# The opening of a hybrid encoder block: first half of the input in 512 KB pairs and scaled by its norm ahead, modulated forms from ScalarE, adaLN row sums in a PSUM bank a piece ahead

## The chip, the cores and the metric

One of the eight cores of one Trainium2 chip runs the kernel; the other seven are idle. The metric is the time of one execution in microseconds (us), as the median of three runs. A core has five engines that run on their own and wait for one another by semaphores: TensorE (PE in the profile, with its weight loads as PEld), VectorE (DVE), ScalarE (ACT), GpSimd (POOL) and SyncE (SP), which issues nearly all DMAs of this kernel.

## The reference

One encoder block of width 1024 over a sequence of 1024 positions, batch 1, in float32. What the change touches is its first lines: a conditioning vector `c` gives six vectors of 1024 (`ada`), the input is normalised and modulated by two of them, and the result goes through one wide projection.

```python
ada = jax.nn.silu(c) @ w_ada[i] + b_ada[i]
shift1, scale1, gate1, shift2, scale2, gate2 = [t[:, None, :] for t in jnp.split(ada, 6, axis=-1)]

h = rmsnorm(x, g_mix[i]) * (1 + scale1) + shift1
proj = h @ w_in[i]
qa, ka, va, qb, kb, vb, ga, gb = jnp.split(proj, split_at, axis=-1)
...
merged = jax.nn.sigmoid(ga) * ya + jax.nn.sigmoid(gb) * yb
x = x + gate1 * (merged @ w_out[i])
h2 = rmsnorm(x, g_ffn[i]) * (1 + scale2) + shift2
...
return rmsnorm(x, g_final)
```

`rmsnorm` divides each position by the root of the mean of its squares and multiplies by a gain. Behind the projection stand a dilated attention of three patterns, a neighbourhood attention on a 16 x 64 grid, two branch products with sigmoid gates, an output product, and a ConvFFN of 2 x 2816 columns.

## The kernel before, in words

The input comes transposed: `xT` is eight blocks `k` of 128 channels by 1024 positions, and the positions are treated in two halves of 512. Every float32 product is made of three products of rounded parts: an operand is split into a high part `hi` and the rest `lo`, and PE adds hi by hi, hi by lo and lo by hi in one PSUM bank. `split` does this for weights (ScalarE copies the high part, `tensor_tensor` on VectorE or GpSimd subtracts it), `modulate` for the activations.

The opening, which is the first 63 us, does this:

1. Load the first half of the input, `x[0]` (eight tiles of 256 KB), and square it (`square`: ScalarE squares, VectorE adds four tiles into each of two sums). PE sums over the channels by products with a column of ones (`add_sums`, 128 x 1 products), `rstd_of` makes 1/root, and `bcast` spreads it over the partitions of a PSUM bank, `pb`. Idle products of the identity with itself (`warm`) stand between these steps on PE.
2. The adaLN product for the first two vectors is cut into four pieces `q` of 512 columns: two blocks `k` of shift and the same two blocks of scale. A piece of `w_ada` is 1024 rows, eight tiles `t` of 128 rows by 512 columns. Six of the tiles are multiplied by their column of `silu(c)` (`cs`) and added up by VectorE (`ada_rows`, a `tensor_scalar` and five `scalar_tensor_tensor`, in place in the first tile). PE does the other two tiles and the sum over partitions of the added ones, four 128 x 1 products for each (`ada_sums`, into the bank `pada`). `piece_bias` adds the bias and makes `1 + scale` times the gain for two blocks.
3. `modulate` makes, for each block, `t = x * am1 * pb` (VectorE, into a PSUM bank), `hi = t + shift` (ScalarE), `lo = t + shift - hi` (VectorE).
4. As soon as two blocks are there, PE adds their part to two banks of q and k (`qk_products`, 512 columns wide) and to four half banks of v (`v_products`, 256 wide). Then comes the next piece.

Everything in this opening stands in one block with a fixed order (`manual_schedule`): each engine runs its instructions in the order in which the code is written, and so does the SP queue with its loads. What sets the time is therefore which instruction stands ahead of which on an engine. Steps 2 to 4 go once for each of the four pieces, in the loop `for q in range(4)`. Behind it stand the same steps for the second half of the input, `x[1]`, whose norm and modulation lie beside products of the first half.

Buffers: `x[0]` and `x[1]` lie in tiles of the pool `h`, the pieces of `w_ada` in tiles that later hold q and k (`kl`, `qs`, `ks`, `qb`) or in tiles named `wada`. The split weights of q and k come in halves of four blocks (`qk_split(0)`, `qk_split(1)`, from tiles `wraw` into `whi` and `wlo`), and those of v likewise (`v_split`, into `vwh` and `vwl`).

## Time and profile before

| | us |
|---|---|
| median of three runs | 1534.29 (1532.61 to 1536.65) |
| the profiled execution, its own time | 1535.67 |
| its span in the profile | 1533.8 |
| PE busy in the span | 1494.4 (97%) |
| VectorE, ScalarE, GpSimd busy | 994.6, 771.6, 774.2 |
| first product of q and k starts (L84) | 25.84 |
| last of the four pieces ends, the second half of v starts (L244) | 62.74 |
| mean clock granted to PE over the span | 0.99 |

All times inside the execution are us from the start of the span. A row of the timeline gives start, length (of the whole group, where several are merged), engine, line, operation, what it writes and reads, the count, and in brackets the idle time of the engine before it with what ended it. In a row of `x16` at line 153 or 98 each 128 x 1 float32 product counts twice, since PE makes two passes of it. A row of the windows gives the stretch, its length, the busy time of each engine with the number of instructions, the granted PE clock (1.00 is full), the DMA share and GB/s; a row of PE alone has only its own busy time. Products are pipelined: a row of 0.39 for a 512-wide product does not mean that the next one starts 0.39 later.

### The profile page before, as it was taken

Reading aid. Unit: us, or ns where it says so; the run is one execution under the profiler, and the core shown is the slowest. Engines: PE = TensorE matmul, PEld = TensorE weight load, DVE = VectorE, ACT = ScalarE, POOL = GpSimd, SP = SyncE. Lnnn points to the kernel's source line nnn. Section 1 sums busy time; section 2 is a strip of 40 time slices with the busy share of each in tenths; the row PEclk is TensorE's granted clock in tenths of the full one; section 3 lists DMA queues with packets and bytes.
Section 4 is the critical chain, followed back from the end, with each engine's and each line's share of the span. In section 5 each row is a group of like instructions: output and inputs, shape, how many; then the busy total and the mean of one; then the engine's idle time right before and its main releaser. Section 6 shows DMA issues by size and latency. Waiting matters only on the chain.

```text
span 1533.8 us, 21797 instructions
## 1 busy us (share of the span) xinstructions
PE 1494.4 (97%) x7740; PEld 1267.5 (83%) x7740; DVE 994.6 (65%) x1892; ACT 771.6 (50%) x1439; POOL 774.2 (50%) x640
## 2 busy tenths in 40 slices
PE   8999999999999999999999989999999998999998
PEld 7888888889798998878888867888888887778787
DVE  5775357575656655646525798766666668787765
ACT  4331566666656566643335463444444447475542
POOL 1021344443335444512268578676666666779721
PEclk9999999999999999999999999999999999999999
DMA  9567333333625456477644222222222224513313
GB/s 349 191 242 258 93 107 82 108 90 102 185 83 150 128 143 173 149 246 234 213 137 147 88 69 96 82 98 88 85 84 86 86 78 154 191 62 124 117 55 111
DMA packets 112725, 205.77 MB, mean 134 GB/s; under 512 B 40516, under 2 KB 53188, under 8 KB 112580
## 3 DMA queue, kind: packets, MB, share of 16 engines
q1 hardware_dynamic: 112344, 204.12, 41.2%
q8 instruction: 61, 1.00, 0.3%
q14 instruction: 48, 0.39, 0.1%
q10 hardware_dynamic: 272, 0.26, 0.1%
HBM read 159.25 MB, written 42.47 MB: 132 GB/s over the span
## 4 chain that ended last, share of the span: by engine, by line
PE 50%; POOL 8%; DVE 7%; ACT 3%; issue 3%; DMA 3%; DVEq 0%; POOLq 0%; ACTq 0%
PE pj L1204 8%; PE pj L1205 8%; PE pj L1206 8%; PE pj L84 6%; PE pj L86 6%; PE pj L85 6%; POOL wsl L61 2%; DMA wraw<-w_down 2%; PE pj L365 2%; PE O L932 2%; POOL wlo L61 2%; DVE big L1426 1%; PE T L919 1%; PE S L897 1%; DVE kl L340 1%
## 5 line engine op out<-in xcount | busy, mean ns | idle before, releaser
L61 POOL TENSOR_TENSOR wlo<-wraw,whi 128x512 fp32r<-128x512 f32 (+1 forms) x94 | 116.1, 1256 | 173.6 <-ACT whi L57 155.4
L84 PE MATMUL pj<-h,whi 128*128 128x512 f32 x448 | 186.7, 417 | 2.6 <-ACT h L207 2.2
L85 PE MATMUL pj<-h,whi 128*128 128x512 f32 x448 | 176.5, 394 | 2.1 <-DVE h L209 2.1
L86 PE MATMUL pj<-h,wlo 128*128 128x512 f32 x448 | 176.3, 393 | 0.0
L61 POOL TENSOR_TENSOR wsl<-big,wsh 128x512 fp32r<-128x512 f32 (+1 forms) x86 | 116.6, 1376 | 43.4 <-ACT wsh L57 43.4
L639 POOL TENSOR_TENSOR wlo<-wraw,whi 128x512 fp32r<-128x512 f32 x58 | 74.7, 1298 | 118.4 <-ACT whi L638 118.4
L589 DVE TENSOR_TENSOR tl<-T,th 128x512 fp32r<-128x512 f32 (+3 forms) x120 | 77.1, 653 | 72.9 <-ACT th L588 71.4
L581 ACT ACTIVATE P<-P,st 128x256 f32<-128x256 f32 x128 | 64.2, 502 | 95.9 <-DVE st L580 95.9
L1426 DVE SCALAR_TENSOR_TENSOR big<-wc,sm,big 128x256 f32<-128x256 f32 (+1 forms) x129 | 101.0, 827 | 15.1 <-ACT big L1420 15.1
L86 PEld LDWEIGHTS pj<-h,wlo 128*128 128x128 f32 x448 | 84.3, 188 | 18.7
L84 PEld LDWEIGHTS pj<-h,whi 128*128 128x128 f32 x448 | 85.0, 190 | 14.3 <-ACT h L207 2.8
L85 PEld LDWEIGHTS pj<-h,whi 128*128 128x128 f32 x448 | 85.0, 190 | 13.4 <-DVE h L209 3.4
L57 ACT ACTIVATE whi<-wraw 128x1024 fp32r<-128x1024 f32 (+2 forms) x51 | 49.5, 972 | 69.8 <-PE pj L85 26.7
L61 POOL TENSOR_TENSOR wsl<-wraw,wsh 128x384 fp32r<-128x384 f32 (+1 forms) x46 | 53.6, 1184 | 58.4 <-ACT wsh L57 58.3
L910 POOL TENSOR_SCALAR P<-P,stb 128x288 f32<-128x288 f32 (+1 forms) x32 | 40.2, 1255 | 72.2 <-DVE stb L907 64.7
L1426 DVE SCALAR_TENSOR_TENSOR big<-pj,sm,big 128x512 f32<-128x512 f32 (+1 forms) x129 | 66.4, 563 | 15.7 <-ACT big L1420 15.7
L588 ACT ACTIVATE th<-T 128x512 fp32r<-128x512 f32 (+3 forms) x120 | 65.6, 566 | 20.4 <-PE T L919 14.0
L57 ACT ACTIVATE wsh<-big 128x1024 fp32r<-128x1024 f32 (+1 forms) x43 | 42.9, 997 | 57.3 <-POOL big L1155 43.0
L547 POOL TENSOR_TENSOR vv<-vv 128x512 fp32r<-128x512 f32 (+1 forms) x40 | 41.9, 1065 | 47.2 <-ACT vv L546 47.2
L580 DVE CUSTOM_DVE_ANT_0 P<-S,bias 128x256 f32<-128x256 f32 x128 | 48.9, 419 | 21.4 <-PE S L692 17.0
L903 ACT ACTIVATE P<-P,stb 128x288 f32<-128x288 f32 (+1 forms) x64 | 36.4, 569 | 50.3 <-DVE stb L901 50.2
L1225 DVE TENSOR_TENSOR pj<-pj,wc 128x512 f32<-128x512 f32 x33 | 22.9, 695 | 53.1 <-PE pj L1206 53.1
(431 smaller groups left out, 4814.3 us busy)
## 6 DMA issues: line engine op xcount, KB each, us to landing
wraw<-w_in SPq DMA_DIRECT2D x34, 512.0 KB, 4.3
wada<-w_ada SPq DMA_DIRECT2D x31, 512.0 KB, 8.0
big<-w_up SPq DMA_DIRECT2D x22, 512.0 KB, 5.4
wraw<-w_up SPq DMA_DIRECT2D x22, 512.0 KB, 3.7
as<-big SPq DMA_DIRECT2D x22, 512.0 KB, 2.8
big<-as SPq DMA_DIRECT2D x22, 512.0 KB, 6.7
wraw<-w_down SPq DMA_DIRECT2D x24, 384.0 KB, 3.6
gs<-gs SPq DMA_DIRECT2D x32, 256.0 KB, 2.9
```

Of the source, the lines that this page charges most:

```text
L57: act.activation(hi, raw, AF.Copy)
L61: lo_eng.tensor_tensor(lo[:, i:i + step], raw[:, i:i + step], f(hi)[:, i:i + step], OP.subtract)
L84: pe.matmul(psum, whi[:, k0 + k], mhi, start=k == 0, stop=False)
L85: pe.matmul(psum, whi[:, k0 + k], mlo, start=False, stop=False)
L86: pe.matmul(psum, wlo[:, k0 + k], mhi, start=False, stop=k == n - 1)
L588: act.activation(th[:m, :n], pt[:m, :n], AF.Copy)
L589: dve.tensor_tensor(tl[:m, :n], pt[:m, :n], f(th)[:m, :n], OP.subtract)
L639: pool.tensor_tensor(lo[:, i:i + n], raw[:, i:i + n], f(hi)[:, i:i + n], OP.subtract)
L1204: pe.matmul(psum, whi[:, k], bhi, start=j < 4 and k == 0, stop=False, skip_group_check=True)
L1205: pe.matmul(psum, whi[:, k], blo, start=False, stop=False, skip_group_check=True)
L1206: pe.matmul(psum, wlo[:, k], bhi, start=False, stop=k == n - 1, skip_group_check=True)
L1426: dve.scalar_tensor_tensor(y[:, dst], src, wt, y[:, dst], OP.mult, OP.add)
```

## The change

All of it lies in the opening, but for the last load of `x` near the end, which follows the new layout of the input in memory (by halves, then pairs of blocks).

- Loads: the first half of the input comes as four pairs of 512 KB with 4 KB a partition, into tiles of q and k (`ks`, `qb`); the small `idt` and `cs` are issued by ScalarE's queue. Pieces 1 and 2 of `w_ada` go to `wada` and `qb` tiles, piece 3 to eight tiles of the pool `h`, one row tile to a load. The second weights of v (`v_raw1`) are loaded ahead of the second half of the input, into free tiles.
- Norm: two of the eight squares go to PE as they are, so VectorE adds four times instead of six. The broadcast norm `pb` is copied to SBUF (`pbs`), and `x[0]` itself is multiplied by it ahead of the modulation: blocks 0 to 3 by VectorE from PSUM, 4 to 7 by GpSimd from `pbs`.
- Modulation: `scaled` lets ScalarE make both `hi = x * am1 + shift` and the same value unrounded into a PSUM bank; VectorE only subtracts.
- Row sums: `ada_rows` adds in a PSUM bank `acc` and writes the last sum to a tile. Pieces 2 and 3 add seven tiles on VectorE and leave one to PE, and their first two or three rows are added a piece ahead.
- Order on PE: `qk_products` goes hi by hi, hi by lo of the weight, then lo of the activation, over both banks; `v_parts` goes by parts. The row sums of the next piece stand behind 6 of the 24 products of v, where they stood behind 12 (in the first piece they stand around the first 8). The idle products are 14, 2, 4 and 4 where they were 28, 8, 4 and 12.
- Splits: the second halves of the weights of q, k and v go from VectorE to GpSimd, and of the second weights of v one goes to VectorE and one to GpSimd, in the last piece.

```diff
@@ -40,10 +40,10 @@
         return ap.bitcast(FT)
 
     idt = const.tile([128, 128], FT, name="idt")
-    sp.dma_start(idt, ident)
+    nc.scalar.dma_start(idt, ident)
     sm = const.tile([128, 248], FT, name="sm")
     cs = const.tile([128, KT], FT, name="cs")
-    sp.dma_start(cs, c)
+    act.dma_start(cs, c)
     ones = const.tile([128, 1], FT, name="ones")
     dve.memset(ones, 1.0)
     ada = const.tile([128, 48], FT, name="ada")
...
@@ -141,6 +140,12 @@
             wt = wada_tile(j)
             sp.dma_start(wt, w_ada[j][:, t:t + 2])
             rows += [wt[:, i] for i in range(2)]
+        return rows
+
+    def ada_rows_load(j):
+        rows = [h_tile(FT) for _ in range(KT)]
+        for t, w in enumerate(rows):
+            sp.dma_start(w, w_ada[j][:, t])
         return rows
 
     def ada_sums(parts, pa=None, stop=True, n=4, new=None):
@@ -159,20 +164,26 @@
         cc = slice(c0, c0 + n)
         dve.tensor_tensor(ada[:, cc], pa[:, :n], b_ada[:, cc], OP.add)
 
-    def ada_rows(wt, ts, acc=None):
+    def ada_rows(wt, acc, ts, first, last):
 
         for t in ts:
-            if acc is None:
-                acc = wt[t]
-                dve.tensor_scalar(acc, acc, cs[:, t:t + 1], None, OP.mult)
+            col, dst = cs[:, t:t + 1], wt[t] if t == last else acc
+            if t == first:
+                dve.tensor_scalar(dst, wt[t], col, None, OP.mult)
             else:
-                dve.scalar_tensor_tensor(acc, wt[t], cs[:, t:t + 1], acc, OP.mult, OP.add)
-
-    def x_load(hf, ks=range(KT)):
+                dve.scalar_tensor_tensor(dst, wt[t], col, acc, OP.mult, OP.add)
+
+    def x_load(hf):
         x = []
-        for k in ks:
-            x.append(h_tile(FT))
-            sp.dma_start(x[-1], xT[k][:, halves[hf]])
+        for k in range(0, KT, 2):
+            if hf == 0:
+                x2k = qkpool.tile([128, 2, 512], FT, name=("ks", "qb")[k // 6], bufs=(4, 2)[k // 6])
+                sp.dma_start(x2k, xT[hf, k // 2])
+                x += [x2k[:, i] for i in range(2)]
+            else:
+                for i in range(2):
+                    x.append(h_tile(FT))
+                    sp.dma_start(x[-1], xT[hf, k // 2][:, i])
         return x
 
     def sq_accs():
@@ -208,6 +219,14 @@
             if last:
                 dve.scalar_tensor_tensor(*last, OP.add, OP.subtract)
             last = k is not None and (lo, t, b, f(hi))
+
+    def scaled(x, k):
+
+        hi, lo = h[0, k] = h_tile(), h_tile()
+        t, b, g = stage[k % 2], ada[:, k:k + 1], am1[:, k:k + 1]
+        act.activation(hi, x, AF.Identity, bias=b, scale=g)
+        act.activation(t, x, AF.Identity, bias=b, scale=g)
+        return lambda: dve.tensor_tensor(lo, t, f(hi), OP.subtract)
 
     def warm(n, dst, fresh=False):
 
@@ -283,8 +302,21 @@
 
     def qk_products(ks):
         for k in ks:
-            for p, w in zip(qk_psum, qk_w):
-                product(p, w, lambda k: h[0, k], ks=[k])
+            mhi, mlo = h[0, k]
+            for x_, (part, m) in enumerate(((0, mhi), (1, mhi), (0, mlo))):
+                for p, w in zip(qk_psum, qk_w):
+                    pe.matmul(p, w[part][:, k], m, start=k + x_ == 0, stop=k == KT - 1 and x_ == 2)
+
+    def v_parts(hv, sts, ks, parts):
+        whi, wlo = v_w[hv]
+        for part in parts:
+            for st in sts:
+                p = pvs[hv][st]
+                sc = slice(st * 128, st * 128 + 128)
+                for k in ks:
+                    m, w = ((0, whi), (1, whi), (0, wlo))[part]
+                    pe.matmul(p, h[0, k][m][:, sc], w[:, k], start=part + k + st % 2 == 0,
+                              stop=part == 2 and k == KT - 1, skip_group_check=True)
 
     def v_products(hv, sts, ks):
         for st in sts:
@@ -391,53 +423,83 @@
         half_load(qk_raw, (0, 4), 1)
         half_load(v_raw, (8, 9), 1)
         wt.append(ada_load(2))
-        wt.append(ada_load(3))
+        wt.append(ada_rows_load(3))
+        v_raw1 = [qkpool.tile([128, KT, 128], FT, name=n) for n in ("kl", "qs")]
+        for t, raw in enumerate(v_raw1):
+            sp.dma_start(raw, w_in[10 + t])
         x.append(x_load(1))
         qk_w = [[wpool.tile([128, KT, 128], FR, name=n) for n in ("whi", "wlo")] for _ in range(2)]
         v_all = v_tiles()
         v_w = [[t[:, hv] for t in v_all] for hv in range(2)]
         qk_psum = [ps_g.tile([128, 512], FT, name="pj") for _ in range(2)]
-        first = ps_s.tile([128, 512], FT, name="pv", bufs=3)
-        stage = [None, first]
-
-        warm(28, first[:, :128], True)
+        acc = ps_s.tile([128, 512], FT, name="pv", bufs=3)
+        pvs = [v_banks()]
+        idle = pvs[0][0][:, :128]
+
+        warm(14, idle, True)
         accs = sq_accs()
-        square(x[0], accs, range(8), dve)
-        pcol = square_sums(accs, lambda: warm(8, first[:, :128], True))
-        ada_rows(wt[0], range(3))
+        square(x[0], accs, range(6), dve)
+        last = [early.tile([128, 512], FT, name="mt", bufs=3) for _ in range(2)]
+        for sq, xk in zip(last, x[0][6:]):
+            act.activation(sq, xk, AF.Square)
+        pcol = ps_n.tile([128, KT], FT, name="pcol")
+        for i, sq in enumerate(accs + last):
+            add_sums(pcol, sq, i == 0, i == 3)
+            if i == 0:
+                warm(2, idle, True)
+        ada_rows(wt[0], acc, range(3), 0, 5)
         rs = rstd_of(pcol, 4)
-        warm(4, first[:, :128], True)
+        warm(4, idle, True)
         pb = bcast(rs, ps_n, "pbc")
-        ada_rows(wt[0], range(3, 6), wt[0][0])
+        pbs = early.tile([128, 512], FT, name="mt", bufs=3)
+        act.activation(pbs, pb, AF.Copy)
+        ada_rows(wt[0], acc, range(3, 6), 0, 5)
+        for k in range(2):
+            dve.tensor_tensor(x[0][k], x[0][k], pb, OP.mult)
+        qk_split(0, (pool, pool))
         pa = ada_sums([(wt[0][t], cs[:, t:t + 1]) for t in (6, 7)], stop=False)
-        ada_sums([(wt[0][0], ones)], pa)
-        warm(12, first[:, :128], True)
-        stage[0] = ps_n.tile([128, 512], FT, name="pcol")
-        qk_split(0, (pool, pool))
-        v_split(v_raw, (pool, pool), slice(0, 4), v_w[0])
-        pvs = [v_banks()]
+        ada_sums([(wt[0][5], ones)], pa)
+        warm(4, idle, True)
         for q in range(4):
             ks = range(2 * q, 2 * q + 2)
-            if q == 2:
-                v_raw1 = v_load(0, 1)
             piece_bias(q, pa)
-            modulate(x[0], 0, ks, pb)
-            qk_products(ks)
-            if q < 3:
-                ada_rows(wt[q + 1], range(6))
             if q == 0:
-                qk_split(1, (dve, dve))
-                v_split(v_raw, (dve, dve), slice(4, 8), v_w[0])
-            if q == 2:
-                v_split(v_raw1, (dve, dve), slice(0, KT), v_w[1])
+                for k in range(2, 4):
+                    dve.tensor_tensor(x[0][k], x[0][k], pb, OP.mult)
+                stage = [ps_n.tile([128, 512], FT, name=n) for n in ("pcol", "pbc")]
+            low = [scaled(x[0][k], k) for k in ks]
+            if q == 0:
+                v_split(v_raw, (pool, pool), slice(0, 4), v_w[0])
+                for k in range(4, 8):
+                    pool.tensor_tensor(x[0][k], x[0][k], pbs, OP.mult)
+            if q == 1:
+                qk_split(1, (pool, pool))
+                v_split(v_raw, (pool, pool), slice(4, 8), v_w[0])
+            last = 6 if q else 5
+            steps = (range(q + 1, 4), range(4, 5), range(5, 7)) if q else (range(0), range(2), range(2, 6))
+            for some, then in zip(steps, low + [None]):
+                if q < 3:
+                    ada_rows(wt[q + 1], acc, some, 0, last)
+                if then:
+                    then()
+            if q < 2:
+                ada_rows(wt[q + 2], acc, range(q + 2), 0, 6)
             if q == 3:
+                v_split(v_raw1, (dve, pool), slice(0, KT), v_w[1])
                 accs = sq_accs()
                 square(x[1], accs, range(8), dve)
-            v_products(0, (0, 1), ks)
+            qk_products(ks)
+            if q == 0:
+                pa = ada_sums([(wt[1][t], cs[:, t:t + 1]) for t in (6, 7)], stop=False)
+                v_parts(0, range(4), ks, (0,))
+                ada_sums([(wt[1][5], ones)], pa)
+                v_parts(0, range(4), ks, (1, 2))
+                continue
+            v_parts(0, (0,), ks, range(3))
             if q < 3:
-                pa = ada_sums([(wt[q + 1][t], cs[:, t:t + 1]) for t in (6, 7)], stop=False)
-                ada_sums([(wt[q + 1][0], ones)], pa)
-            v_products(0, (2, 3), ks)
+                pa = ada_sums([(wt[q + 1][7], cs[:, 7:8])], stop=False)
+                ada_sums([(wt[q + 1][6], ones)], pa)
+            v_parts(0, (1, 2, 3), ks, range(3))
         pairs = [(j, i) for j in range(4, 10) for i in range(4)]
         rows = {n: pair_load(*pairs[n]) for n in range(7)}
         for st in range(4):
@@ -1107,7 +1169,7 @@
-            sp.dma_start(x2[hf][-1], xT[m][:, cols])
+            sp.dma_start(x2[hf][-1], xT[hf, m // 2][:, m % 2])
@@ -1730,7 +1792,7 @@
-        "xT": x[0][_POS].T.reshape(KT, 128, S),
+        "xT": x[0][_POS].T.reshape(4, 2, 128, 2, 512).transpose(3, 0, 2, 1, 4),
```

The order on PE ahead of the first product, before. L98 are the sums of squares, L111 the broadcast, L153 the row sums of the first piece, L215 idle products:

```order
L215 MATMUL pv<-idt 128x128 x28
L98 MATMUL pcol<-ones,sq 128x1 x4
L215 MATMUL pv<-idt 128x128 x8
L98 MATMUL pcol<-ones,sq 128x1 x4
L215 MATMUL pv<-idt 128x128 x4
L111 MATMUL pbc<-idt,rs 128x128 x4
L153 MATMUL pada<-cs,qs 128x1 x8
L153 MATMUL pada<-ones,kl 128x1 x4
L215 MATMUL pv<-idt 128x128 x12
```

And now, where L234 is the idle product and L158 the row sum:

```order
L234 MATMUL pv<-idt 128x128 x14
L98 MATMUL pcol<-ones,sq 128x1 x4
L234 MATMUL pv<-idt 128x128 x2
L98 MATMUL pcol<-ones,sq 128x1 x4
L98 MATMUL pcol<-ones,mt 128x1 x8
L234 MATMUL pv<-idt 128x128 x4
L111 MATMUL pbc<-idt,rs 128x128 x4
L158 MATMUL pada<-cs,qs 128x1 x8
L158 MATMUL pada<-ones,qs 128x1 x4
L234 MATMUL pv<-idt 128x128 x4
```

There are 28 idle products fewer, and eight more sums of squares.

The order on VectorE for the second piece of the opening, before: the bias of the piece (L272, L274), the modulation of two blocks (L206, L209), and the rows of the third piece (L167, L169):

```order
L272 TENSOR_TENSOR ada<-pada,sm 128x2x2
L274 SCALAR_TENSOR_TENSOR am_71<-ada,sm 128x2
L206 SCALAR_TENSOR_TENSOR pcol<-h,am_71,pbc 128x512
L206 SCALAR_TENSOR_TENSOR pv<-h,am_71,pbc 128x512
L209 SCALAR_TENSOR_TENSOR h<-pcol,ada,h 128x512
L209 SCALAR_TENSOR_TENSOR h<-pv,ada,h 128x512
L167 TENSOR_SCALAR wada<-wada,cs 128x512
L169 SCALAR_TENSOR_TENSOR wada<-wada,cs 128x512 x5
```

And now, from the first rows of the third piece (L172, L174, ahead of the second piece's bias L291) to the first rows of the fourth (`pv<-h`), with the two low parts (L229) between the rows:

```order
L172 TENSOR_SCALAR pv<-wada,cs 128x512
L174 SCALAR_TENSOR_TENSOR pv<-wada,cs,pv 128x512
L291 TENSOR_TENSOR ada<-pada,sm 128x2x2
L293 SCALAR_TENSOR_TENSOR am_71<-ada,sm 128x2
L174 SCALAR_TENSOR_TENSOR pv<-wada,cs,pv 128x512 x2
L229 TENSOR_TENSOR h<-pcol,h 128x512
L174 SCALAR_TENSOR_TENSOR pv<-qb,cs,pv 128x512
L229 TENSOR_TENSOR h<-pbc,h 128x512
L174 SCALAR_TENSOR_TENSOR pv<-qb,cs,pv 128x512
L174 SCALAR_TENSOR_TENSOR wada<-wada,cs,pv 128x512
L172 TENSOR_SCALAR pv<-h,cs 128x512
L174 SCALAR_TENSOR_TENSOR pv<-h,cs,pv 128x512 x2
```

Between bias and low part two row steps stand instead of the first modulation step, and the bias itself stands behind two rows of the next piece.

The order on ScalarE at the start, now (L196 and L444 are squares, L286 the sigmoid of `c`, L104 the root):

```order
L43 DMA idt<-ident 128x128
L46 DMA cs<-c 128x8
L196 ACT_TABLE_LOAD
L196 ACTIVATE sq<-ks 128x512
L286 ACT_TABLE_LOAD
L286 ACTIVATE rs<-cs 128x8
L196 ACTIVATE mt<-ks 128x512 x3
L196 ACTIVATE sq<-ks 128x512
L196 ACTIVATE mt<-ks 128x512
L444 ACTIVATE mt<-qb 128x512 x2
L104 ACT_TABLE_LOAD
L104 ACTIVATE rs<-rs 128x4
```

Before, one table was loaded ahead of the sigmoid and kept for the squares; now a first one is loaded for the first square and a second one for the sigmoid behind it.

5 lines of the change are left out of this document (2 added, 3 removed).

## The prediction

> **What bounds the kernel now.** I read the windows first, then the timelines of PE and VectorE, then the waits.
>
> ```profile
> 0.00:20.00 20.00, 16.23 (x121) 15.44 (x121) 8.74 (x16) 9.28 (x14) 1.47 (x6) 0.98 0.83 299
> 20.00:40.00 20.00, 17.45 (x99) 15.76 (x99) 14.34 (x25) 6.06 (x10) 3.67 (x3) 0.85 1.03 402
> 40.00:60.00 20.00, 18.28 (x125) 16.22 (x124) 16.97 (x27) 7.53 (x12) 0.00 (x0) 1.00 0.72 260
> 60.00:80.00 20.00, 20.00 (x157) 19.39 (x156) 13.31 (x22) 9.20 (x18) 0.00 (x0) 1.00 0.26 75
> ```
>
> The first busy column is PE. Up to 60 us PE has holes; from there it is full (20.00 of 20). What arrives earlier at the end of the fourth piece therefore shortens the whole execution by as much, as long as PE stays full behind it. So I predict that moment, 62.74 before.
>
> ```profile
> 17.34 1.95 PE L153 MATMUL pada<-cs,qs 128*128 128x1 f32 x16 [0.53 <-DMA qs<-w_ada]
> 19.15 1.71 PE L153 MATMUL pada<-ones,kl 128*128 128x1 f32 x8
> 20.72 5.47 PE L215 MATMUL pv<-idt 128*128 128x128 f32 x24
> 22.08 0.69 ACT L207 ACTIVATE h<-pcol,ada 128x512 fp32r<-128x512 f32 x1 [0.31 <-DVE pcol L206]
> 25.84 0.61 PE L84 MATMUL pj<-h,whi 128*128 128x512 f32 x1
> 26.22 0.76 DVE L206 SCALAR_TENSOR_TENSOR pv<-h,am,pbc 128x512 f32<-128x512 f32 x1 [4.18 <-PE pv L215]
> ```
>
> The last pair of the first `w_ada` piece lands at 17.3, its sums end at 20.86, and the first `hi` is there at 22.77. But PE is in its twelve idle products until 26.2, and they hold a bank that VectorE waits 4.18 for. They run at half clock:
>
> ```profile
> 12.83:16.24 3.41, 2.81 (x24) 1.00 1.03 410
> 16.24:19.65 3.41, 2.88 (x23) 0.95 1.05 392
> 19.65:23.07 3.42, 3.42 (x17) 0.50 1.03 410
> 23.07:26.48 3.41, 3.38 (x16) 0.55 1.04 393
> ```
>
> These are windows of PE alone, cut at the clock's steps of 3.41. The clock falls to 0.50 at 19.66, behind a window that shows 2.88 busy but holds only the broadcast and 128 x 1 products, and returns after one full window at half clock. So 128 x 1 products hardly count as activity here.
>
> ```profile
> 37.06 0.50 PE L84 MATMUL pj<-h,whi 128*128 128x512 f32 x1 [1.03 <-ACT h L207]
> 37.84 0.50 PE L85 MATMUL pj<-h,whi 128*128 128x512 f32 x1 [0.28 <-DVE h L209]
> 51.47 1.84 PE L153 MATMUL pada<-cs,wada 128*128 128x1 f32 x16
> 53.17 1.03 PE L153 MATMUL pada<-ones,wada 128*128 128x1 f32 x8
> 56.45 0.49 PE L84 MATMUL pj<-h,whi 128*128 128x512 f32 x1 [0.72 <-ACT h L207]
> 57.58 0.39 PE L86 MATMUL pj<-h,wlo 128*128 128x512 f32 x1
> 59.87 0.28 PE L244 MATMUL pv<-vwh,h 128*128 128x256 f32 x1
> 62.74 0.28 PE L244 MATMUL pv<-vwh,h 128*128 128x256 f32 x1
> 65.62 1.84 PE L98 MATMUL pcol<-ones,sq 128*128 128x1 f32 x16
> ```
>
> A piece on PE: ten wide products from 57.58 to 59.87 are 0.229 each, so twelve are 2.75; the 24 of v are 2.87 (59.87 to 62.74); the 24 passes of row sums about 2.7. Four products and three sums are 30.6 of the 36.9 from 25.84 to 62.74; 6.3 is waiting: each piece waits for its first `hi`, then for its first `lo`.
>
> **The change, part by part.**
>
> *Loads ahead of the first product.*
>
> ```profile
> 0.72 0.39 SPq L43 DMA_DIRECT2D idt<-ident  x1
> 1.63 4.04 SPq L175 DMA_DIRECT2D h<-xT  x8
> 0.71 1.28 ACT L267 ACT_TABLE_LOAD   x1 [0.71 <-PEq L1760]
> 4.00:6.00 2.00, 2.00 (x13) 2.00 (x12) 0.00 (x0) 0.95 (x2) 0.00 (x0) 1.00 0.57 189
> 12.00:14.00 2.00, 1.95 (x18) 1.76 (x17) 1.86 (x3) 1.82 (x2) 0.00 (x0) 1.00 1.03 416
> 10.56 1.98 ACT L185 ACTIVATE mt<-h 128x512 f32<-128x512 f32 x3
> ```
>
> With `idt` and `cs` on ScalarE's queue, SP issues `x` at 0.72 instead of 1.63. The last square before starts at 11.9, so the last tile landed by then. While `x` loads, the DMA engines move 189 GB/s where 416 go later. If that stays as it is, the last pair lands 0.9 earlier, at 11.0; if four longer loads fill the engines at once, 2.1 MB need 5.2, and it lands near 9.1 with the landing delay. I take 10.4, nearer the first. The later table load (1.28) ends near 6, hidden behind that wait, and so are the two issues (0.4 each) that ScalarE now makes ahead of it. All later loads follow in a full queue (402 GB/s): the first piece lands at 15.9, the third near 32.
>
> *Sums of squares, norm, row sums.*
>
> ```profile
> 13.56 1.05 PE L98 MATMUL pcol<-ones,sq 128*128 128x1 f32 x8
> 15.50 0.16 DVE L103 TENSOR_SCALAR rs<-pcol 128x4 f32<-128x4 f32 x1
> 16.16 0.65 PE L111 MATMUL pbc<-idt,rs 128*128 128x128 f32 x4 [0.55 <-DVE rs L105]
> 16.02 2.29 DVE L169 SCALAR_TENSOR_TENSOR kl<-qs,cs,kl 128x512 f32<-128x512 f32 x3
> ```
>
> The last squares are done at 11.6. Three groups of sums (24 passes) stand there now: 1.05 each at full clock, 1.71 at half (the row at 19.15). With 14 idle products the dense work ends near 7.5, so a sparse window follows surely and the clock falls between 9.4 and 13: sums end between 13.8 and 15.7, I take 15.0. Root and reciprocal take 0.66. The four idle products are eight passes at half clock, 5.47 / 24 = 0.23 each, so PE is free at 16.8, and the broadcast, at twice 0.65 at most, ends at 17.9. Row sums: 24 passes at 0.21 (1.71 / 8) are 5.1, to 23.0, where they ended at 20.86 before. VectorE is not late: rows three to five (2.29) and two products by `pb` (0.7 each) end by 19.7. Bias 0.4, `hi` 0.7: there at 24.1. The four idle products hold PE until 24.8. **First product at 24.8, 1.0 earlier**; the bounds are 19.5 (full clock all along, `x` at 9.1) and 27 (half clock from 9.4, `x` at 11.9).
>
> *First piece.* PE is dense from 23.0, so the clock returns after one to two windows, near 28.1. Until then seven products of 0.45 run, then five of 0.23: 29.2. Row sums 2.7 and v 2.9 bring 34.8, and 0.3 for the bias, which now waits behind two rows of the third piece. VectorE's six rows of the second piece end near 31, GpSimd's `vwl` near 27, both in time.
>
> *Second to fourth piece.* The next bias (0.4) and `hi` (0.7) lie beside 18 products of v, 2.15: the wait for `hi` is covered. If that cover goes, it costs the 0.4 to 1.0 of before. The wait for `lo` is covered by four products that need only `hi`. Row sums fall from 24 passes to 16, 1.8. A piece costs 2.75 + 2.87 + 1.8 = 7.4, two of them 14.8, the fourth 5.6. So the fourth piece ends at 24.8 + 4.4 + 2.7 + 2.9 + 0.3 + 14.8 + 5.6 = **55.5, 7.2 earlier**.
>
> *Is VectorE in time for that?* Per piece it does bias 0.35, two low parts 1.4 and seven row steps.
>
> ```profile
> 28.40 0.48 DVE L167 TENSOR_SCALAR ks<-ks,cs 128x512 f32<-128x512 f32 x1
> 28.91 3.90 DVE L169 SCALAR_TENSOR_TENSOR ks<-ks,cs 128x512 f32<-128x512 f32 x5
> L1091 DVE SCALAR_TENSOR_TENSOR pcol<-oraw,cs,pcol x12: 747/747/756, 685.4 to 757.7; 128x512 f32<-128x512 f32 x12
> ```
>
> A row step goes every 0.78 in SBUF; L1091, the same sum in a PSUM bank, takes 0.75 of its own, like L169. So nothing is won by the bank itself, and seven rows are 5.2; the sum, 6.9, is just under PE's 7.4. ScalarE's four modulated forms (2.8) and splits (2.3) fit too.
>
> *Behind the opening.* `v_raw1`'s splits and the squares of `x[1]` come later against PE than before: ScalarE finishes the squares near 57, VectorE's sums near 59.5, and PE asks for the second at 59. I charge 0.4. On SP's queue `v_raw1` now stands ahead of `x[1]`, which costs `x[1]` 1 MB at 402 GB/s, 2.6: it lands near 46, and ScalarE asks for it near 52. The layout of the last load of `x` changes no size and costs nothing.
>
> **Sum:** 7.2 - 0.4 = 6.8. The profiled execution took 1535.67 with a span of 1533.8 and would take 1528.9; the median is 1.4 lower: 1534.3 - 6.8 = **1527.5**.
>
> **The rivals.**
>
> *The clock stays up.* Then the sums of squares end at 13.8, the row sums at 18.7 behind the landing at 15.9, the first product starts near 20.5 and the first piece takes no half-clock: 4.3 + 1.7 = 6 more, 1521.5; since the third piece's loads (near 32) then bind, I give it 1523. For it speaks that no hole on PE would be longer than 3. The Trainium skill, page TensorE: Matmul & The Clock Gate, section on HAM oscillation, says just this: the clock is lost by idle gaps of over some 3 us. By that sentence PE stays at full clock and this rival holds. The trace disagrees: the window at 16.24 shows 2.88 of 3.41 busy, and the clock fell.
>
> *The opening gains nothing before the first product.* If `x` lands as before and the clock is low from 9.4, the first product comes at 27, 1.2 late instead of 1.0 early: gain 4.6, 1529.7. If, beside that, VectorE is late by 0.5 a piece, 1531.5: no change.
>
> *GpSimd and VectorE block each other: slower.* GpSimd gets twelve steps by 36 us where it had four.
>
> ```profile
> 105.55 1.78 DVE L61 TENSOR_TENSOR vwl<-wraw,vwh 128x512 fp32r<-128x512 f32 x1
> 106.74 1.74 POOL L61 TENSOR_TENSOR vwl<-wraw,vwh 128x512 fp32r<-128x512 f32 x1
> 21.18 2.49 POOL L61 TENSOR_TENSOR vwl<-kl,vwh 128x512 fp32r<-128x512 f32 x2
> 21.29 0.76 DVE L206 SCALAR_TENSOR_TENSOR pcol<-h,am,pbc 128x512 f32<-128x512 f32 x1
> ```
>
> Side by side, both L61 take 1.75 where they take 0.65 and 1.25 alone. If row steps suffered likewise, twelve meetings would add 12 x (1.78 - 0.78) = 12 to VectorE, which has 0.5 to spare a piece: 1527.5 + 11 = 1538.5 to 1540. It decides from 6.8 / 12, some 0.55 more per step. Against it: L206, with one operand in PSUM, took its 0.76 beside the L61 of 21.18, and all new steps of VectorE but one have an operand in PSUM. The Trainium skill (SBUF — State Buffer, two separate sides) names two SBUF inputs as the condition; the two pairs of rows agree.
>
> **How the numbers follow.** The forecast gets 0.50 (own range 1525 to 1530), the clock that stays up 0.20, no gain ahead of the first product 0.20, the blocking 0.10. A measurement of this kernel tells a change from none beyond about 0.3%, 4.6. Faster by more than that: 0.45 of the first case, all of the second, 0.07 of the third: 0.72. Slower: 0.08 of the last; the rest, 0.20, within. The range takes in the second case and the third: 1521.5 to 1532.5.
>
> **What would show it.** In the new profile: the clock at 0.50 from before 13 to about 28; the first wide product near 24.8; row sums of 16 passes behind six products of v; no waits on PE of over 0.4 between pieces; the second half of v at 55.5; row steps of 0.75 to 0.78 beside GpSimd. Wrong would make me: row steps of over 1.3, a third piece of `w_ada` that lands behind 33, or holes on PE behind 60.

## The result and the profile after

The changed kernel takes 1529.54 us in the median of 13 runs (1526.37 to 1532.2), the one before 1533.07 (1530.51 to 1536.65, 13 runs on the same chip): a ratio of 0.9976 (0.9967 to 0.9985), 3.5 us less. The forecast was 1527.5, with a range of 1521.5 to 1532.5. Three later measurements, one of the same kernel and two of it with one small edit in the opening, gave 0.9965 to 0.9970, about 4.6 to 5.4 us; the ratios together stand near 0.997. The forecast gain was 6.8. The ratios given here and below are not exactly the quotients of the medians.

The profiled execution took 1528.78 (span 1527.0). Its windows, PE's busy time first:

```profile
0.00:20.00 20.00, 15.49 (x99) 15.30 (x99) 8.81 (x16) 10.16 (x16) 2.68 (x6) 0.87 0.91 350
20.00:40.00 20.00, 19.84 (x123) 17.75 (x123) 18.12 (x29) 9.55 (x15) 12.49 (x10) 0.87 1.04 396
40.00:60.00 20.00, 18.94 (x132) 17.39 (x133) 11.93 (x19) 13.17 (x24) 3.10 (x2) 0.98 0.65 250
60.00:80.00 20.00, 20.00 (x119) 18.26 (x119) 17.87 (x27) 8.66 (x16) 0.00 (x0) 0.93 0.23 60
```

From 20 us on PE has 1.2 us of holes in 40, where it had 4.3. The granted clock is lower in three of the four windows, though: 0.87, 0.87, 0.98 and 0.93 stand where 0.98, 0.85, 1.00 and 1.00 stood. The rows of PE that answer to those of before:

```profile
4.22 5.26 PE L234 MATMUL pv<-idt 128*128 128x128 f32 x28 [4.22 <-DMA idt<-ident]
12.02 1.93 PE L98 MATMUL pcol<-ones,mt 128*128 128x1 f32 x16
15.42 3.41 PE L158 MATMUL pada<-cs,qs 128*128 128x1 f32 x16
22.11 1.20 PE L308 MATMUL pj<-h,whi 128*128 128x512 f32 x2
40.32 0.73 PE L308 MATMUL pj<-h,whi 128*128 128x512 f32 x2 [0.46 <-ACT h L227]
53.96 0.28 PE L263 MATMUL pv<-vwh,h 128*128 128x256 f32 x1
58.34 1.05 PE L98 MATMUL pcol<-ones,sq 128*128 128x1 f32 x8 [0.55 <-DVE sq L198]
69.89 0.40 PE L275 MATMUL pj<-vwh,h 128*128 128x512 f32 x1
```

The last of them before, where the line is 256:

```profile
76.47 0.40 PE L256 MATMUL pj<-vwh,h 128*128 128x512 f32 x1
```

The first product starts at 22.11 (25.84 before), the pieces follow at 31.95, 40.32 and 48.34 (37.06, 46.62, 56.45), and the second half of v starts at 53.96 (62.74): 8.8 earlier. The first 512-wide product of v, L275, starts at 69.89 where it started at 76.47: 6.6 earlier. So 2.2 are lost between 54 and 70, at the wait of 58.34 and the clock behind it.

### The profile page after: what moved, and what is told of

It is laid out like the page before. It is cut to its first block, busy times and chain, and to the rows that moved or that the text cites. A ratio compares the mean times of both kernels' runs of the same rounds, so it can differ in the third digit from the quotient of the medians.

```text
span 1527.0 us, 21705 instructions
## 1 busy us (share of the span) xinstructions
PE 1490.2 (98%) x7684; PEld 1263.1 (83%) x7684; DVE 990.6 (65%) x1883; ACT 778.0 (51%) x1449; POOL 786.9 (52%) x650
## 4 chain that ended last, share of the span: by engine, by line
PE 72%; DVE 9%; DMA 6%; ACT 5%; POOL 5%; issue 3%; SPq 1%; DVEq 0%; POOLq 0%; ACTq 0%
PE pj L1268 10%; PE pj L1267 10%; PE pj L1266 10%; PE pj L84 9%; PE pj L86 9%; PE pj L85 9%; PE pj L397 3%; PE O L994 2%; DVE big L1488 1%; DMA wada<-w_ada 1%; DMA wraw<-w_in 1%; PE T L981 1%; PE O L828 1%; PE S L959 1%; POOL wsl L61 1%
## 5 line engine op out<-in xcount | busy, mean ns | idle before, releaser
L84 PE MATMUL pj<-h,whi 128*128 128x512 f32 x432 | 179.5, 416 | 1.4 <-ACT gs L1041 1.1
L86 PE MATMUL pj<-h,wlo 128*128 128x512 f32 x432 | 169.8, 393 | 0.0
L85 PE MATMUL pj<-h,whi 128*128 128x512 f32 x432 | 169.5, 392 | 0.0
L86 PEld LDWEIGHTS pj<-h,wlo 128*128 128x128 f32 x432 | 81.1, 188 | 18.1
L84 PEld LDWEIGHTS pj<-h,whi 128*128 128x128 f32 x432 | 81.5, 189 | 12.4 <-ACT gs L1041 1.5
L85 PEld LDWEIGHTS pj<-h,whi 128*128 128x128 f32 x432 | 81.8, 189 | 9.5
L642 DVE CUSTOM_DVE_ANT_0 P<-S,bias 128x256 f32<-128x256 f32 x128 | 48.9, 419 | 21.5 <-PE S L754 17.1
```

The source lines that it names most:

```text
L84: pe.matmul(psum, whi[:, k0 + k], mhi, start=k == 0, stop=False)
L85: pe.matmul(psum, whi[:, k0 + k], mlo, start=False, stop=False)
L86: pe.matmul(psum, wlo[:, k0 + k], mhi, start=False, stop=k == n - 1)
```

## Experiments

In the expectation of after_again, A says that more time at half clock takes part of the gain back, B that the profiled execution of the old kernel took longer than it typically does, C that later stages lose it. In those of before_again and before_idle_4_again, D says that the phase of the clock decides what the idle products cost. Elsewhere a theory is what its own text says. A step that all kernels share behind the opening (ScalarE's `P<-P,st`, line 581 before, 643 after) measures the opening in each trace. Before:

```profile
194.73 0.51 ACT L581 ACTIVATE P<-P,st 128x256 f32<-128x256 f32 x1 [1.39 <-DVE st L580]
```

and in the changed kernel:

```profile
187.90 0.51 ACT L643 ACTIVATE P<-P,st 128x256 f32<-128x256 f32 x1 [1.40 <-DVE st L642]
```

| run | median us (runs) | ratio to before (95%) | that step against 194.73 |
|---|---|---|---|
| after_again | 1528.61 (12) | 0.9968 (0.9954 to 0.9983) | -5.7 |
| after_idle_3 | 1528.42 (12) | 0.9965 (0.9953 to 0.9977) | -4.7 |
| x_singles | 1528.53 (6) | 0.9970 (0.9958 to 0.9981) | -6.6 |
| sums_apart | 1527.78 (8) | 0.9957 (0.9938 to 0.9976) | -7.7 |
| not_ahead | 1529.94 (12) | 0.9982 (0.9970 to 0.9994) | -5.7 |
| rows_in_sbuf | 1536.91 (12) | 1.0013 (1.0001 to 1.0025) | -0.5 |
| idle_52 | 1532.91 (12) | 0.9988 (0.9975 to 1.0001) | -1.8 |
| before_idle_4, and its second trace | 1529.97 (12) | 0.9970 (0.9957 to 0.9984) | -1.9, -2.3 |
| before_idle_30 | 1532.32 (12) | 0.9995 (0.9984 to 1.0005) | -0.2 |
| before_again | 1536.86 (1) | | -0.5 |
| best1 | 1537.27 (11) | 1.0030 (1.0018 to 1.0042) | -6.5 |

**The two kernels again, unchanged.**

> The changed kernel unchanged, for a second trace and the clock of each run. Theory A (the opening gains 8 to 9 us, and a typical run gives part of it back to half clock, which the sparse stretches of the new order bring about): 3 to 4.5 us faster than the kernel before on the same chip; the second half of v starts 8 to 9.5 us earlier than 62.74; the runs of the changed kernel spend 33 to 37 us at half clock, those of the kernel before 5 us less. Rival B (the profile of before was a slow draw, the opening gains only some 4 us in a typical run): the second half of v starts 4 to 6 us earlier, half-clock time is the same within 2 us. Rival C (the gain is real and lost in later stages): the second half of v starts 8 to 9 us earlier, the clock is the same, and a stage behind 90 us is 3 us or more longer.

> The kernel before unchanged, for a second trace of its opening. By the means of the runs so far (span 1532.0 of 31 runs before, 1528.2 of 12 with 4 idle products, 1527.4 of 25 changed) the opening must vary from run to run with the moment at which the clock falls. Theory D (the phase of the clock decides what the twelve idle products cost: 2.8 us at full clock, 5.5 at half): the first wide product lies between 22.8 and 25.9, and v's first wide product between 73 and 77. Rival (the opening is the same in each run, the spread comes from later stages): 25.8 and 76.5 within 0.3 us.

The changed one shows the step 5.7 earlier, where the first pair of traces had 6.8; the old one shows 0.5. The second half of v starts at 56.35, 6.4 before 62.74: more than B's 4 to 6, less than the 8 to 9.5 of A and C. C falls, since at 1290 us the lead is still 5.7 (6.9 in the changed kernel's first trace). The old kernel's first product comes at 25.07 and its first 512-wide product of v at 75.84, both within D's range; but the clock fell there at 19.25 as it did at 19.31 in the first trace, so it was not its phase that moved them.

Over whole runs the half clock took 32.1 us on average in the old kernel and 32.1 in the changed one beside it (35.3 in the changed kernel's first runs); on another chip it took 31.7 in the old kernel, 33.6 in after_idle_3 and 35.1 in x_singles. So the 5 us more that A asked for did not come; 0 to 3.4 did, which is at most 1.7 of time. In the openings A holds in part: up to the step the old traces (with before_idle_30) have 6.8 to 10.2 us at half clock, those of the new opening (with after_idle_3 and x_singles) 10.2 to 17.1 and of these the one with 17.1 (after_idle_3) comes latest.

**The idle products.** One number of the old kernel is changed, and, the other way round, the changed kernel is given the old counts.

```diff
# before_idle_4, before_idle_4_again
-        warm(12, first[:, :128], True)
+        warm(4, first[:, :128], True)
# idle_52
-        warm(14, idle, True)
+        warm(28, idle, True)
...
-                warm(2, idle, True)
+                warm(8, idle, True)
...
-        warm(4, idle, True)
+        warm(12, idle, True)
```

> The kernel before with 4 idle products instead of 12 ahead of the first wide product, nothing else. By the rows of before: the idle products end at 20.72 + 8 x 0.23 = 22.6, the first hi is there at 22.77, so the first wide product starts near 22.8 instead of 25.84; at half clock until 26.5 it gives back 1.5: 1 to 2 us faster than the kernel before. Rival (the idle products pay for the clock): the clock stays at 0.50 a window longer, and the time is within 0.5 us of the kernel before or above it.

> The kernel before with 4 idle products, a second trace. Its first trace had its first wide product at 22.72 and half clock from 22.0 to 28.8, with v's first wide product at 74.35; its mean span asks for some 72.2. Theory D: where the half clock falls elsewhere, the first piece takes 9.7 instead of 11.8 us, and v's first wide product comes at 71 to 73. Rival (it is always as in the first trace): 74.3 within 0.5 us.

> The changed kernel with the idle products of before: 28, 8, 4, 12 for 14, 2, 4, 4. Theory A: idle products delay more than a full clock saves. They start at 4.2, so 28 end near 12.5, the sums of squares near 18, the first wide product comes near 25 instead of 22.1, the first piece runs at full clock and takes back 1.7: 1 to 2.5 us slower than the changed kernel. Rival (the clock is what counts): the clock stays at 1.00 from 8 us on, and it is 1 to 3 us faster.

The old kernel's first product moves to 22.72 and now waits for its `hi`:

```profile
19.74 1.14 PE L215 MATMUL pv<-idt 128*128 128x128 f32 x8
22.72 0.79 PE L84 MATMUL pj<-h,whi 128*128 128x512 f32 x1 [1.84 <-ACT h L207]
```

In idle_52 the products meant for a waiting PE stand in the way instead:

```profile
4.72 8.92 PE L234 MATMUL pv<-idt 128*128 128x128 f32 x56 [4.72 <-DMA idt<-ident]
13.48 0.95 PE L98 MATMUL pcol<-ones,sq 128*128 128x1 f32 x8
25.27 5.30 PE L234 MATMUL pv<-idt 128*128 128x128 f32 x24
```

The sums of squares start 3.7 later than with 14 (9.77), and the last twelve products hold PE for 5.3. The first wide product comes at 30.32 (22.11), and the clock, which the rival saw at 1.00 from 8 us on, is at half from 20.0 to 30.3. Fewer idle products are worth 3.4 us on the old kernel by the medians (1533.39 in its runs beside it, to 1529.97), 1.9 and 2.3 by the step of the table. On the changed one they are worth 3.4 to 4.3 by the medians (1532.91 against 1528.61 and 1529.54), 1.8 to 3.1 by the ratios. More of them saved little half clock: 32.1 with twelve and 34.4 with four on the old kernel, 34.2 with 52 and 32.1 to 35.3 with 24 on the changed one, on average. The second trace of before_idle_4 has v's first 512-wide product at 74.18 where the first had 74.35: the rival to D had that within 0.5, D had 71 to 73.

**The bank, and the piece ahead.**

```diff
# rows_in_sbuf
-        acc = ps_s.tile([128, 512], FT, name="pv", bufs=3)
+        acc = early.tile([128, 512], FT, name="accs", bufs=1)
# not_ahead
-            steps = (range(q + 1, 4), range(4, 5), range(5, 7)) if q else (range(0), range(2), range(2, 6))
+            steps = (range(0, 4), range(4, 5), range(5, 7)) if q else (range(0), range(2), range(2, 6))
...
-            if q < 2:
-                ada_rows(wt[q + 2], acc, range(q + 2), 0, 6)
```

> The changed kernel with the running sum of w_ada rows in SBUF instead of a PSUM bank, all else equal. Theory (a step with both operands in SBUF cannot run beside GpSimd's): row steps beside GpSimd take 1.3 to 1.8 us instead of 0.76, GpSimd's 1.25 become up to 1.75, some ten meetings cost VectorE 6 to 10 us, of which 3 to 7 reach the time. Rival (the bank is no help): row steps stay at 0.75 to 0.8, the time within 0.7 us of the changed kernel.

> The changed kernel with no rows of w_ada added a piece ahead: all seven rows of the third and of the fourth piece stand behind the bias and between the low parts of the piece before. Theory (the sums of a piece end VectorE's row steps just before PE wants them; two or three rows at 0.78 come back into the piece): PE waits 1 to 2 us for the row sums in the second and third piece, 1.5 to 3 us slower than the changed kernel. Rival (VectorE has slack, the bias in front gains what the rows lose): within 0.7 us.

With the sum in SBUF a row step takes 1.6 beside GpSimd (0.75 where GpSimd stands still, as at 48.72), and GpSimd's products by `pbs` slow down with it. PE then waits for the row sums and for the next `hi`. The rows of rows_in_sbuf:

```profile
23.21 4.82 DVE L174 SCALAR_TENSOR_TENSOR accs<-wada,cs,accs 128x512 f32<-128x512 f32 x3
25.77 3.39 POOL L474 TENSOR_TENSOR ks<-ks,mt 128x512 f32<-128x512 f32 x2
29.76 1.87 PE L158 MATMUL pada<-ones,wada 128*128 128x1 f32 x8 [1.28 <-DVE wada L174]
45.27 0.74 PE L308 MATMUL pj<-h,whi 128*128 128x512 f32 x2 [1.75 <-ACT h L227]
```

and of the changed kernel:

```profile
25.14 2.33 DVE L174 SCALAR_TENSOR_TENSOR pv<-wada,cs,pv 128x512 f32<-128x512 f32 x3
26.98 2.52 POOL L474 TENSOR_TENSOR ks<-ks,mt 128x512 f32<-128x512 f32 x2
```

It costs the whole gain: the step comes at -0.5, and the time is 5.7 to 6.9 above the changed kernel's by the ratios, 7.4 to 8.3 by the medians. Part of that is clock: these runs were at half clock for 43.2 us on average, 8 to 11 more than the changed kernel's, which is worth 4 to 5.5.

Taking away the rows a piece ahead costs 0.4 to 1.3 by the medians and 0.9 to 2.1 by the ratios, which the intervals don't tell from nothing. The mechanism of its theory did not come: PE waits nowhere for the row sums of the second and third piece, only 0.89 for a `lo` at 42.81.

**The square sums of `x[1]` apart.** The second group of sums stands a half bank of v later, so that VectorE is done by then.

```diff
-        pcol = square_sums(accs)
+        pcol = ps_n.tile([128, KT], FT, name="pcol")
+        add_sums(pcol, accs[0], True, False)
         v_products(1, (1,), range(8))
+        add_sums(pcol, accs[1], False, True)
+        v_products(1, (2,), range(8))
         pb = bcast(rstd_of(pcol, 4), ps_n, "pbc")
...
-        v_products(1, (2, 3), range(8))
+        v_products(1, (3,), range(8))
```

> The changed kernel with the square sums of the second half apart: the first four 128 x 1 products behind the first quarter of v's second half, the other four behind the second quarter, the broadcast behind the third. Theory A: the wait of 0.55 us at the second sums is gone, the clock no longer falls near 60 us, and it is 1.5 to 2.5 us faster than the changed kernel. Rival (half clock is lost at other places): the wait is gone, the time falls by 0.6 us at most. If the later broadcast makes v's wide products wait for the modulation (there were 3 us to spare): slower by up to 1 us.

Two windows of PE in the changed kernel, cut close to the clock's steps (it falls at 59.37):

```profile
56.20:59.60 3.40, 2.85 (x25) 0.97 0.27 84
59.60:63.01 3.41, 3.41 (x19) 0.53 0.31 94
```

and the same with the sums apart:

```profile
56.20:59.60 3.40, 3.40 (x32) 1.00 0.26 82
59.60:63.01 3.41, 3.41 (x32) 1.00 0.23 77
```

The hole of 0.55 between two groups of 128 x 1 products is gone, and with it the window at half clock. From the second half of v to L275 it is 13.72 here, 13.73 in the old traces, 15.93 in the changed kernel's and 14.45 in after_again, where the wait is there and the clock stays. The median is the lowest of all, 0.6 to 1.8 below the same opening without it; the intervals overlap, so the runs don't tell A's 1.5 to 2.5 from the rival's 0.6, and only the traces show what the wait costs, 0.7 and 2.2.

The hole by itself does not decide. Seven traces have it, and the clock fell behind it in four. In the old kernel it also fell without one; in before_again at 53.38, behind row sums that follow one another closely:

```profile
50.66 1.84 PE L153 MATMUL pada<-cs,wada 128*128 128x1 f32 x16
52.36 1.03 PE L153 MATMUL pada<-ones,wada 128*128 128x1 f32 x8
49.97:53.38 3.41, 3.41 (x33) 1.00 0.53 154
53.38:56.80 3.42, 3.42 (x15) 0.50 0.68 216
```

What decides in these traces is where the products lie. The clock changes at steps of 3.41, which stand elsewhere in each trace. Take the stretches between these steps, from 5 to 85 us in all 14 traces, and add up in each what PE spent on 128 x 1 products and on waits. Of the stretches at full clock, half clock followed all with more than 2.1 us of that and only two others (one of 2.0 in idle_52, and one in rows_in_sbuf with a wait of 1.75). The sums of squares with the hole take 2.55. In four traces they lay in one stretch, but for 0.14 at most; in the other three a step of the clock divided them. Without the hole, as in the old kernel, they take 1.84. This was read from the traces afterwards; no run was made for it.

**Does the late order count?** The ConvFFN's second product is left to a scheduler, and its order in the built program differs between these kernels. From 1290 us to the end single traces gain up to 3.7 us on the first old one, and the question is whether the order is the reason.

```diff
# after_idle_3
         ada_sums([(wt[0][5], ones)], pa)
-        warm(4, idle, True)
+        warm(3, idle, True)
# before_idle_30
-        warm(28, first[:, :128], True)
+        warm(30, first[:, :128], True)
```

> The changed kernel with three idle products instead of four behind the row sums, where PE waits for the first `hi` anyway. Built so, the ConvFFN's second product, whose order nobody writes by hand, has word for word the order of the kernel before; the changed kernel has another one (245 of its some 6,600 rows on PE stand elsewhere, all between 1300 and 1470 us). Theory E, the order of that stage is a term of its own: up to 1290 us the trace runs as the changed one's (5.7 to 6.9 ahead of the old trace), and from there to the end it gains nothing more on the old trace (-0.3 to +1.1, as the traces that share that order do), where the changed kernel's gained 0 to 2.4; the mean span is about 3.5 below the old one's, ratio 0.9977. Rival F, that stage's differences are luck from run to run: the same as the changed kernel in every respect, ratio 0.997, and a late gain anywhere between 0 and 4.

> The old kernel with 30 idle products instead of 28 in its first row, most of it beside the wait for the input; the opening should be the old one within 0.5 us. Built so, the ConvFFN's second product takes the order that the old kernel with four idle products had (203 rows of PE elsewhere than in the old order). Theory E: at 1290 us it stands where the old trace stands (0 to 0.5), and behind it gains 2.8 to 3.7, as both traces with that order did; total about 2 below the typical old run, ratio 0.998 or less. Then half of what the edit from twelve to four idle products gained was this order and not the idle products. Rival F: no late gain that stands out from the old traces (within 1.1), ratio 1.000.

Behind 1290 the first gained 1.3 where E expected -0.3 to 1.1, and the second 2.9 as E expected; but x_singles (below), which has the order of the second, gained 1.2 where E expected some 3. Over all runs the changed opening stands at 0.9968, 0.9965 and 0.9970 in three late orders, and the old opening at 0.9995 in the second order. So E is not borne out, though the last interval leaves up to 2.5 us: what single traces show there is mostly the run. Against before_idle_30, which has its late order, before_idle_4 is 2.35 lower by the medians and 3.8 by the ratios, measured on different chips; its opening gained 2.

**The loads of `x`.**

```diff
-                sp.dma_start(x2k, xT[hf, k // 2])
-                x += [x2k[:, i] for i in range(2)]
+                for i in range(2):
+                    sp.dma_start(x2k[:, i], xT[hf, k // 2][:, i])
+                    x.append(x2k[:, i])
```

> The changed kernel with the first half of the input loaded in eight loads of 256 KB, 2 KB a partition, into the same tiles, instead of four of 512 KB. It too takes the late order of before_idle_30. If the pairs are what fills the DMA engines at once, `x` arrives as it did before (some 190 GB/s around 5 us instead of 410), the squares end 1 us later and the first product too, which costs 0 to 1 by the second piece, since that is bound by the half clock and the third piece's load. Theory E beside that: a late gain of some 3 behind 1290 us, so 6 to 7 below the typical old run, ratio 0.9955 to 0.996. Rival F: ratio 0.997 to 0.9975. If the pairs do nothing, the rate at 4 to 8 us is 410 here too, and what filled the engines was that the loads were issued 0.9 earlier.

From 6 to 8 us, the window of the changed kernel (the last number is GB/s):

```profile
6.00:8.00 2.00, 2.00 (x11) 2.00 (x11) 0.74 (x2) 1.99 (x5) 0.00 (x0) 1.00 1.01 411
```

and of x_singles:

```profile
6.00:8.00 2.00, 2.00 (x11) 2.00 (x11) 1.44 (x3) 1.14 (x4) 0.00 (x0) 1.00 0.83 263
```

The pairs fill the engines, and no gain from it shows here: the step comes at -6.6 without them and the median is the same. Twice as many loads also hold up the queue, which issues the first load of `w_ada` at 5.43 instead of 3.25; the run does not tell that apart from the size.

**`am` without two operands in SBUF**, on top of the sums apart.

```diff
-        dve.scalar_tensor_tensor(am1[:, ks], cc[0][:, 1], 1.0, g_mix[:, ks], OP.add, OP.mult)
+        dve.tensor_tensor(pa[:, 2:4], pa[:, 2:4], g_mix[:, ks], OP.mult)
+        dve.tensor_tensor(am1[:, ks], pa[:, 2:4], bg[:, ks], OP.add)
...
+    bg = const.tile([128, KT], FT, name="bg")
...
+        dve.scalar_tensor_tensor(bg, b_ada[:, 8:16], 1.0, g_mix, OP.add, OP.mult)
```

> The kernel with the square sums of `x[1]` apart, and `am` made without a VectorE step that reads two operands from SBUF: the gain is multiplied into the bank `pada` first and a prepared product of bias and gain is added from there. Such a step of 128 x 2 took up to 1.02 us beside GpSimd instead of 0.16, ahead of the first `hi` of a piece. If two SBUF operands are the cause, both new steps take 0.2 or less in every piece, the wait of 0.4 to 0.5 ahead of the third piece goes, and the first product comes 0.5 earlier than with the sums apart (19.7 in a phase with full clock up to 19.6); 0.5 to 1 us in all up to 1290 us. If it is the read of a small operand beside GpSimd as such, they stay at up to 1. The late order is another one here (that of the row sums in SBUF, which gained 1.1 behind 1290 us): theory E gives a late gain near 1 and a ratio of 0.996, rival F the same 0.9957 as with the sums apart, or 0.995.

The third piece's step in the changed kernel:

```profile
38.33 1.02 DVE L293 SCALAR_TENSOR_TENSOR am<-ada,sm 128x2 f32<-128x2 f32 x1
```

with GpSimd's split beside it:

```profile
36.81 2.52 POOL L61 TENSOR_TENSOR vwl<-kl,vwh 128x512 fp32r<-128x512 f32 x2
```

and in best1, beside the same split:

```profile
38.10 0.17 DVE L294 TENSOR_TENSOR pada<-pada,sm 128x2 f32<-128x2 f32 x1
38.31 0.16 DVE L295 TENSOR_TENSOR am<-pada,bg 128x2 f32<-128x2 f32 x1
```

That part came as expected, in all four pieces, and L275 starts at 66.85, the earliest of all. The first product did not come at 19.7, since the clock fell at 14.9 in this trace, but at 21.88. And the kernel is slower than the old one by 0.3%, for the most part in a place nobody touched. Between 1000 and 1290 PE is busy for 287.2 of 290 us in the changed kernel and for all 290 in best1. A group of the ConvFFN's products of the changed kernel (busy time, mean ns of one):

```profile
L1267 PE MATMUL pj<-T2lo,wsh 128*128 128x512 f32 x60 | 23.3, 389 | 0.0
```

and the same group, with another one, of best1:

```profile
L1273 PE MATMUL pj<-T2lo,wsh 128*128 128x512 f32 x60 | 23.7, 396 | 0.0
L1274 PE MATMUL pj<-B21hi,wlo 128*128 128x512 f32 x60 | 23.3, 389 | 0.0
```

The granted clock is 1.00 in both. Between 960 and 1290 best1 goes from 3.9 ahead of the old trace to 3.9 behind it; it stood 6.5 ahead at the step of the table. The trace of rows_in_sbuf, which has the same late order, lost 0.3 there. What is left is an idea: `bg` takes 32 bytes a partition of the constants, so other tiles can lie 32 bytes further. Groups with the weights `wsh`, `wsl` and `big` take 396 in best1, those with `whi` and `wlo` 389 to 392. The traces hold no addresses and no run moved the tiles alone, so the cause is not shown.

## Why the prediction was right, and where not

- **The fourth piece, 55.5.** The four traces of the new opening (after, after_again, after_idle_3, x_singles) start the second half of v at 53.96, 56.35, 56.06 and 54.94, 55.3 on average; three traces of the old one at 62.74, 62.11 and 62.56. So 7.2 was forecast and 7.1 came on average, with 6.1 to 8.5 in single traces. That mean is close to the forecast in part by luck, as the next point shows. VectorE kept up, with row steps of 0.75 to 0.78 beside GpSimd, and the cover of the next `hi` by products of v held but for 0.46 at the third piece, which was `am` (above).
- **Ahead of the first product** the terms were off and made up for each other. The last squares were done at 10.5, not 11.6, as the bound of filled DMA engines had it; `idt` came later, so the idle products began at 4.22 instead of 2.64; the row sums ended at 20.4, not 23.0, because the clock fell later (15.0 in this trace, not 9.4 to 13) and the sums of squares ran at full clock. In after_again, where it fell at 12.5, they ended at 22.8. Half clock lasted to 25.2 to 27.4 in the four traces, not to 28. The first product came at 22.11 to 24.48, not 24.8, the first piece took 9.6 to 10.0 where 10.3 was forecast, and the two pieces behind it 8.0 to 8.7 each where 7.4 was: there stand the waits of 0.46 for `hi` and 0.20 for `lo`, and without these, in sums_apart, it is 7.5 and 7.7. In sums_apart, with the clock up to 19.2, the first product is at 20.22 and the second piece still at 32.77, since the half clock then falls on the first piece's products. That is why the first rival, the clock that stays up, did not come: nowhere did it stay up through the opening.
- **Behind the opening, 0.4.** This is the step that failed. The late squares of `x[1]` cost 0.7 in every trace (a wait of 0.55) and 2.2 in two of four, where the clock falls behind the wait: 1.5 on average. Of the 7.1 at the fourth piece 5.7 are left at L275. The prediction priced the wait and not what a wait beside 128 x 1 products does to the clock, although it had shown that effect in the old trace (it put the fall at 19.66, where it cut its windows; the granted clock falls at 19.31).
- **From 5.7 to 4.6.** What goes between there and the median's gain lies within what runs of one kernel differ by; no stage was found that loses it. The references of the sum were part of it. The forecast of 1527.5 rests on a median of three runs, 1534.3; from the 1533.07 of the 13 runs beside the changed kernel the same 6.8 would have given 1526.3, so of the forecast gain about half came in the first comparison and two thirds to four fifths in the later ones. And two profiles of the old kernel took 1535.67 and 1536.86, its median is 1533 to 1534, and the two pairs of unchanged kernels, one execution of each, differ by 6.9 and 9.3.
- **"Nothing is won by the bank itself"** was wrong. The row step was compared by itself, 0.75 in PSUM against 0.78 in SBUF. Beside GpSimd it is 0.78 against 1.6, and without the bank the gain is gone. So the third rival's mechanism is real, with a price of 0.8 a step, above the 0.55 from which it was said to decide; the condition that spoke against it, an operand in PSUM, held. The Trainium skill (SBUF — State Buffer, two separate sides) names two SBUF inputs of a VectorE step, against a GpSimd step that reads SBUF, as a condition; these runs agree, with 1.6 against 0.78.
- **The chances.** Faster by over 0.3% had 0.72. The first comparison is just within that bound, the later ones at or just beyond it.
- **Not tested apart:** the splits moved to GpSimd, the two modulated forms on ScalarE and the new order on PE. That they cover the waits of the old pieces is read from the traces.

## What to carry to other kernels

Idle products that keep a clock up have to end before the work they wait for is ready; count them against the wait, since here they delayed work and saved at most some 2 us at half clock. Groups of 128 x 1 products are better spread between wide ones than put together, above all where PE would wait between them. Where GpSimd and VectorE work at the same time, keep one operand of VectorE's steps in PSUM, the small ones in front of a wait too. A small edit at the start can move a later stage that it doesn't touch: compare the same step in both traces before and after each stage, and take the gain from repeated runs, since single pairs of executions were off by 2 and by almost 5 us here.

## What the runs showed of the hardware

- A VectorE step over 128 x 2 elements with both inputs in SBUF took 1.02 instead of 0.16 beside a GpSimd `tensor_tensor`, and ended with it. With one input in PSUM it took 0.16.
- Two groups of 128 x 1 products with a hole of 0.55 on PE between them were followed by a window of 3.41 at half clock in four of seven traces; with wide products between the groups the clock held in both traces. In before_again it fell at 53.38 behind a window in which PE was busy for all of its 3.41, 2.73 of that with 128 x 1 products. The Trainium skill (TensorE: Matmul & The Clock Gate, HAM oscillation) speaks of idle gaps of over some 3 us; here far less sufficed.
- Loads of 256 KB with 2 KB a partition moved 263 GB/s at 6 to 8 us, pairs of 512 KB with 4 KB a partition 411, into the same tiles on the same queue, which the single loads kept busy for longer.
- In best1, which has 32 bytes more a partition in its pool of constants, many of the ConvFFN's 128 x 512 products took 396 instead of 389 ns at a granted clock of 1.00, and 7.8 us were lost between 960 and 1290; why is open.
